# Two mixers of a hybrid decoder trunk: evacuating queries and values from PSUM at once, an order of products per mixer, and new places in the planner's queues

## The chip, the cores and the metric

The kernel runs as one program on one core of a Trainium2 chip. The metric is the device time of one execution in microseconds (us). Three runs of the kernel before took 2170.38, 2173.52 and 2178.13 us; the median is 2173.52. A change of less than 0.3% can't be told from none here.

## The reference

The reference is one inference step of a trunk of two layers with a width of 1024, for 16 meta tokens, a prompt of 512 tokens and eight running sequences of four tokens each: 560 token columns in all. Everything is float32. One layer does this:

```
h = h + 0.5 * swiglu(rmsnorm(h, norm_ffn1), ...)            # 1024 -> 2816 -> 1024
z = rmsnorm(h, norm_mix) @ w_in                             # q, f, v, gate, u: five parts of 512
q = silu(zq); log_f = log(lb + (1-lb) sigmoid(zf)); k = (1-lb) sigmoid(-zf)
o_hg = HGRN2(q, log_f, k, v)        # S_t = diag(f_t) S_{t-1} + k_t v_t^T, o_t = S_t^T q_t; 4 heads of 128
o_hg = rmsnorm(o_hg per head) * silu(zg)
y = gelu(S5(u))                     # complex diagonal scan, 32 groups of 16 columns, 64 states
y = rmsnorm(y * sigmoid(y @ w_glu + b_glu))
h = h + concat(o_hg, y) @ w_out
h = h + 0.5 * swiglu(rmsnorm(h, norm_ffn2), ...)
```

The outputs are the normalised h and the new states of the HGRN2 heads and of the S5 groups, for the prompt and for each running sequence.

## The kernel before

All arrays lie feature-major: a tile has 128 features on its partitions and the 560 tokens beside each other. Each float32 operand of the large products is cut into a high and a low part of a reduced format, and a product is the sum of three (high by high, high by low, low by high). So one product of the mixer with 1024 inputs and 128 outputs is 8 x 3 x 2 = 48 matmuls of 128x128 by 128x280, which add up in a pair of PSUM banks. Weights come from HBM over SyncE's queue (raw) and once more over GpSimd's queue, where the DMA adds the raw weight to a negated high part, so that the low part results; ScalarE makes the high parts.

Four feed-forward stages and two mixers follow each other: feed-forward, mixer 0, two feed-forwards, mixer 1, feed-forward. The feed-forward products use a scheme with seven block products for eight; the change does not touch it beyond its places.

The order of the instructions on the engines is made before the launch by a planner (`Sched`, lines 78 to 288). The work is written as tasks (Python generators), each of which yields one operation after the other, waits for events of other tasks, or asks a pool for a buffer. The planner keeps an estimated clock per engine, and for each engine takes the operation with the smallest key, which is its possible start plus a pull times the task's place:

```
key = st + PULL.get(o.eng, 0.0) * t.prio
if t.slack and o.eng in ("PE", "S"):
    key = max(key, rdy + t.slack)
```

So a place is a handicap in ns for VectorE ("V") and ScalarE ("S"), and none for TensorE and GpSimd. Engines run the emitted instructions in that order and wait at each for what it needs. Some VectorE operations may go to GpSimd (`flex`, line 335) if they end there no later than `BIAS` ns after VectorE would end them.

The pools (line 302) are: `t`, 50 SBUF tiles of 564 columns; `a`, 20 of 1024; `mm`, three pairs of PSUM banks; `m1`, two single banks. In a mixer the main task gets an `mm` pair only where another one stays free (`mtask[0].psum = 1`), so it holds two at most. The S5 and head tasks are ranked: the more of them with a better place are alive (those that wait for a PSUM pair not counted), the more `t` tiles must be free before a task gets one: `RES=(0, 6, 6, 6, 82)`. The fifth one thus gets no tile at all until another ends. A task without that mark needs no free tiles beside its own.

A mixer (`mixer`, line 1846) walks through `ORDER` (line 72), one list for both mixers: `f`, `q`, `v` and `g` with a number are the products of a head, `u` those of one of the four S5 blocks, `x` the two halves of the S5 gate (`w_glu`), which need all four S5 outputs. The weights are loaded in the same order (`wsrc`, line 488). After a product the main task spawns the task that uses it:

- `t_s5` (a block of S5) evacuates u as soon as the norm factor is known, waits for the tables of the layer (`d.ev`), sends u to DRAM and back in another layout, waits for the block before it, and then does a product, a scan on VectorE, a second product and the gelu; y goes to DRAM and back as well.
- `t_head` (line 1568) evacuates f and makes the decay and k, then waits for the q product and evacuates it, waits until the head two before it has done its levels (`prev`), does the first block product, and only then waits for the v product and evacuates it. Seven levels of pairwise decays with a block product each follow, then the states and the output.
- `t_og` applies the gate product to a head's output, `t_glu` the S5 gate, `t_yn` the norm of y. The eight output products come last; each takes the parts of its input in the order in which they are ready.

The tables of a layer's S5 blocks are made by `t_setup` (line 1247 on): some hundreds of short VectorE steps in a chain and some DMA through DRAM. That of layer 0 starts with the kernel, that of layer 1 after mixer 0.

Of the kernel before, what the change touches and what calls it, by code (L numbers as in the profile page):

```python
# [67 lines left out]
BIAS = 1000.0  # L68
# [3 lines left out]
ORDER = 'f0 u0 f1 u1 q0 u2 v0 q1 f2 u3 v1 q2 f3 q3 x0 v3 x1 v2 g1 g3 g2 g0'.split()  # L72
# [4 lines left out]
PULL = {"PE": 0.0, "V": 60.0, "S": 60.0, "G": 0.0}  # L77
# [214 lines left out]
def hymba(ctx: ExitStack, tc: tile.TileContext, *aps):  # L292
# [172 lines left out]
    for l in range(L):  # L465
        for i in ("1", "2"):
            f = 2 * l + int(i) - 1

            def put_units(a, b):
                for k in range(a, b):  # L470
                    unit_at[f, k] = len(wsrc)
                    if f or k >= PLAIN:
                        pair.add(len(wsrc))
                    wsrc.extend([(A_["gu" + i][l, k, 0], 8), (A_["gu" + i][l, k, 1], 8)])

            for a, (c, o, n) in enumerate(CH):
                put_units(ends[a] - n, ends[a])
                down_at[f, a] = len(wsrc)
                if n == 4:
                    wsrc += [(A_["dn" + i][l, c, m:m + 2, :, o:o + 4].rearrange("m p k q -> p m k q"), 8)  # L480
                             for m in range(0, KD, 2)]
                else:
                    wsrc += [(A_["dn" + i][l, c, m, :, :n], n) for m in range(KD)]
            if i == "1":
                m0 = len(wsrc)
                for w, i in ORDER:
                    i = int(i)
                    wsrc.append((A_["wglu"][l, i] if w == "x" else A_["win"][l, WIN[w] + i], 8))
                wsrc += [(A_["wout"][l, m], 8) for m in range(KD)]
                wmix.append((m0, len(wsrc)))  # L490
# [198 lines left out]
    class Norm:  # L689
        def __init__(self, nm, l, src, ev, o0=0, plain=False):  # L690
            self.rs = Ev()
            self.nm, self.l, self.src, self.ev = nm, l, list(src), ev
            self.sq = [Ev() for _ in range(KD)]
            self.o0, self.T = o0, TOK - o0
            self.fast = nm != "nm"
            if self.fast:
                self.xb = {b: [Ev() for _ in range(4)] for b in ("11", "12", "t1", "21", "22", "t2", "t3", "t4")}
                self.xt = []
                self.plain = plain
                self.order = XO if self.plain else range(KD)  # L700
                if self.plain:
                    self.x12, self.y = [], [Ev() for _ in range(KD)]
                    spawn(self.t_first(), 0.931, name="split" + nm)
                    spawn(self.t_then(), 1.2, name="sums" + nm)
                else:
                    spawn(self.t_blocks(), 0.931, name="split" + nm)
            else:
                self.order = range(KD)
                self.xs = [Ev() for _ in range(KD)]
                spawn(self.t_split(), 2.931, name="split" + nm)  # L710
            spawn(self.t_sum(), 1.9 if self.fast else 8.533, name="sum" + nm).slack = 1500.0 if self.fast else 0.0
# [138 lines left out]
    class Unit:  # L850
# [9 lines left out]
        def prod(self, j):  # L860
            w, o, b = PROD[j]
            q, i = wq[self.i], self.i
            if j == 1:
                self.x = yield am1()
                spawn(t_cuts(self), 2.45, name="cuts")
                spawn(t_hid(self), 2.452, name="hid").slack = 400.0
# [21 lines left out]
    class Plain:  # L888
# [4 lines left out]
        def run(self):  # L893
            pss = []
            for n in range(2):
# [13 lines left out]
                if not n:  # L909
                    self.f = Ev()  # L910
                    spawn(t_evac(ps, self.f), 2.45, name="cuts")
            spawn(t_phid(self, ps), 2.452, name="hid")
# [193 lines left out]
    def ffn(nrm, f, nm2, l2=0):  # L1106
# [14 lines left out]
        for u, j in prog:  # L1121
# [30 lines left out]
            for m in range(KD):  # L1152
# [3 lines left out]
                spawn(t_res(pd[m] if m < 2 else p, m, 0.5, hevs[m] if last else Ev(), o0=nrm.o0), 3.536, name="res")  # L1156
# [410 lines left out]

    def t_head(l, hd, st, ps, evs, nrm, prev, nxt, out):
        yield evs[0]
# [10 lines left out]
        yield evs[1]  # L1580
        q = yield from evac(ps[1], rs, "q")
# [33 lines left out]
        yield evs[2]  # L1615
        v = yield from evac(ps[2], rs, "v")
# [229 lines left out]
    def mixer(l, nrm):  # L1846
        spawn(t_park(nrm), 3.523, name="park")
# [17 lines left out]
        spawn(t_ysplit(ys, yh), 8.515, name="ysplit")  # L1865
        spawn(t_yn(l, y2, yf, o0), 2.578, name="yn")
        for w, i in ORDER:
            i = int(i)
            ps = yield am()
            if w == "u":  # L1870
                yield from gemm(ps, list(nrm.xs))
                spawn(t_s5(l, i, st, ps, nrm, nu[i], nu[i + 1], ys[i]), 0.477 + 0.01 * i, 1, name=f"s5{i}")
            elif w == "g":
                yield from gemm(ps, list(nrm.xs), T=TOK - o0, o0=o0)
                spawn(t_og(l, i, ps, nrm, ons[i], ogs[i], o0), 2.926, name="og")
            elif w == "x":
                for j in range(2):
# [3 lines left out]
                    spawn(t_glu(l, 2 * i + j, ps, ys[2 * i + j], y2[2 * i + j]), 2.92, name="glu")  # L1881
# [3 lines left out]
            else:  # L1885
                j = "fqv".index(w)
                hps[i][j] = ps
                if j == 0:
                    spawn(t_head(l, i, st, hps[i], hev3[i], nrm, rel[i], rel[i + 2], ons[i]), 1.202 + 0.01 * i, 1,
# [8 lines left out]
        spawn(t_unpark(back), 9.518, name="unpark")  # L1898
# [4 lines left out]
        for ms in OUT_M:  # L1903
# [9 lines left out]
            while final:  # L1913
# [15 lines left out]
                if n[a] == KD:  # L1929
                    final.remove(a)  # L1930
                    spawn(t_res(pss[a], ms[a], 1.0, hevs[ms[a]], back[ms[a]], o0), 3.536, name="res")
# [7 lines left out]
    def t_main():  # L1939
# [3 lines left out]
        for l in range(L):  # L1943
            nn = yield from ffn(nn, 2 * l, "nm", l)
            nn = yield from mixer(l, nn)
            if l + 1 < L:
                spawn(t_setup(l + 1), 8.527, name="setup")
# [6 lines left out]
    for f, pr in ((t_wload, 0.1), (t_wsplit, 2.311), (t_wsum, 2.312)):  # L1954
        spawn(f(), pr, name=f.__name__[2:])
    spawn(t_ones(), 1.5, name="ones")
    spawn(t_const(), 8.52, name="const")
    spawn(t_mask(), 8.9, name="mask")
    spawn(t_setup(0), 8.527, name="setup")
# [121 lines left out]
```

## Time and profile before

| what | value |
|---|---|
| median of three runs | 2173.52 us |
| the profiled execution's own time | 2174.55 us |
| its span, first to last instruction | 2172.7 us |
| TensorE matmul busy | 2069.9 us (95%) |
| VectorE busy | 1622.1 us (75%) |
| ScalarE busy | 1151.2 us (53%) |
| GpSimd busy | 492.4 us (23%) |
| mean granted TensorE clock | 0.979 of full speed |
| moved by DMA | 388.08 MB, mean 179 GB/s |

The profile is one execution, and times in it count from the first instruction. TensorE's granted clock has two levels, 1.2 and 2.4 GHz, shown as 0.5 and 1.0; a stretch's figure is the mean. A waiting instruction is put down to what released it. Names such as `q<-mm,rs` say what is written from what: here the evacuation of a q product from its PSUM pair, multiplied by the norm factor. `zf`, `v`, `u` and `zg` are the same for the other products, `ut,mi` is the first product of an S5 block, `xh,wh` a piece of a dense one.

### The profile page before, as it was taken

Reading aid. Unit: us, or ns where it says so; the run is one execution under the profiler, and the core shown is the slowest. Engines: PE = TensorE matmul, PEld = TensorE weight load, DVE = VectorE, ACT = ScalarE, POOL = GpSimd, SP = SyncE. Lnnn points to the kernel's source line nnn. Section 1 sums busy time; section 2 is a strip of 40 time slices with the busy share of each in tenths; the row PEclk is TensorE's granted clock in tenths of the full one; section 3 lists DMA queues with packets and bytes.
Section 4 is the critical chain, followed back from the end, with each engine's and each line's share of the span. In section 5 each row is a group of like instructions: output and inputs, shape, how many; then the busy total and the mean of one; then the engine's idle time right before and its main releaser. Section 6 shows DMA issues by size and latency. Waiting matters only on the chain.

```text
span 2172.7 us, 43858 instructions
## 1 busy us (share of the span) xinstructions
PE 2069.9 (95%) x17394; PEld 2019.2 (93%) x17394; DVE 1622.1 (75%) x3654; ACT 1151.2 (53%) x1888; POOL 492.4 (23%) x606
## 2 busy tenths in 40 slices
PE   8999999988699999999999999999988999999997
PEld 7999999987598999999999999999978889999997
DVE  8879769867577977866998865665677797566674
ACT  6556656433354645575765564554434466545563
POOL 2232232322221223123212221112221221111111
PEclk9999999989899999999999999999989999999999
DMA  7798688876456678868857876688856667667773
GB/s 206 162 227 217 154 230 185 235 208 201 109 127 188 151 168 221 196 168 208 191 127 192 217 183 158 154 203 222 216 152 151 164 140 180 169 153 171 183 178 82
DMA packets 153325, 388.08 MB, mean 179 GB/s; under 512 B 16176, under 2 KB 36432, under 8 KB 153120
## 3 DMA queue, kind: packets, MB, share of 16 engines
q0 software_dynamic: 65760, 177.27, 42.6%
q1 hardware_dynamic: 75904, 182.48, 25.4%
q10 hardware_dynamic: 11456, 25.54, 3.4%
q8 instruction: 136, 2.23, 0.4%
q14 instruction: 69, 0.57, 0.1%
HBM read 352.56 MB, written 32.67 MB: 177 GB/s over the span
## 4 chain that ended last, share of the span: by engine, by line
PE 55%; DVE 14%; issue 4%; ACT 2%; DMA 2%; POOL 1%; DVEq 0%; ACTq 0%; POOLq 0%
PE mm L408 38%; PE m L408 16%; DVE xl L333 2%; DVE wr L333 1%; DVE wl L333 1%; ACT wh L372 1%; DMA wl<-in_dn_dram 1%; DVE w L333 1%; DVE fa L333 1%; DMA smin<-mex 1%; DVE w L1523 1%; DVE qp L333 1%; DVE rv L333 1%; DVE ks L333 0%; DVE xh L364 0%
## 5 line engine op out<-in xcount | busy, mean ns | idle before, releaser
L408 PE MATMUL mm<-xh,wh 128*128 128x280 f32 (+1 forms) x3432 | 821.8, 296 | 8.9 <-ACT s L372 3.7
L408 PE MATMUL mm<-xl,wh 128*128 128x280 f32 (+1 forms) x3432 | 809.9, 292 | 6.5 <-DVE xl L333 6.5
L408 PE MATMUL mm<-xh,wl 128*128 128x280 f32 (+1 forms) x3432 | 807.6, 291 | 1.2 <-DMA wl<-in_dn_dram 1.2
L372 ACT ACTIVATE wh<-wr 128x1024 fp32r<-128x1024 f32 (+2 forms) x590 | 524.6, 915 | 285.6 <-DVE wr L333 191.5
L408 PEld LDWEIGHTS mm<-xh,wh 128*128 128x128 f32 x3432 | 577.0, 189 | 23.9 <-issue 7.4
L408 PEld LDWEIGHTS mm<-xl,wh 128*128 128x128 f32 x3432 | 578.6, 189 | 9.4 <-DVE xl L333 9.4
L408 PEld LDWEIGHTS mm<-xh,wl 128*128 128x128 f32 x3432 | 577.9, 189 | 1.7 <-DMA wl<-in_dn_dram 1.7
L408 PE MATMUL m<-xh,wh 128*128 128x280 f32 (+1 forms) x1112 | 310.8, 293 | 1.3 <-ACT fa L372 0.9
L408 PE MATMUL m<-xl,wh 128*128 128x280 f32 (+1 forms) x1032 | 300.9, 292 | 0.4 <-DVE xl L333 0.4
L408 PE MATMUL m<-xh,wl 128*128 128x280 f32 (+1 forms) x952 | 277.6, 292 | 0.3 <-DMA wl<-in_gu_dram 0.3
L372 ACT ACTIVATE wl<-wr 128x1024 fp32r<-128x1024 f32 (+1 forms) x244 | 249.2, 1021 | 40.6 <-PE mm L408 20.2
L333 DVE TENSOR_TENSOR wl<-wr,wh 128x1024 fp32r<-128x1024 f32 x174 | 212.7, 1222 | 54.5 <-PE mm L408 28.5
L333 DVE TENSOR_TENSOR wr<-wr 128x512 f32<-128x512 f32 x344 | 236.0, 686 | 16.3 <-ACT wh L372 13.8
L408 PEld LDWEIGHTS m<-xh,wh 128*128 128x128 f32 x1112 | 206.0, 189 | 4.7 <-issue 2.0
L361 DVE SCALAR_TENSOR_TENSOR h<-mm,h 128x560 f32<-128x560 f32 (+1 forms) x157 | 114.8, 735 | 127.7 <-PE mm L408 126.7
L408 PEld LDWEIGHTS m<-xl,wh 128*128 128x128 f32 x1032 | 195.2, 189 | 0.6 <-DVE xl L333 0.6
L387 POOL DMA_DIRECT2D wl<-in_gu_dram x88 | 77.4, 879 | 522.3 <-ACT wl L372 280.6
L387 POOL DMA_DIRECT2D wl<-in_dn_dram x96 | 103.7, 1082 | 348.2 <-ACT wl L372 131.3
L408 PEld LDWEIGHTS m<-xh,wl 128*128 128x128 f32 x952 | 180.2, 189 | 0.5 <-DMA wl<-in_gu_dram 0.5
L408 PE MATMUL m<-x,wh 128*128 128x280 f32 (+1 forms) x952 | 142.9, 290 | 0.0
L408 PEld LDWEIGHTS m<-x,wh 128*128 128x128 f32 x952 | 129.9, 188 | 0.2 <-issue 0.2
L387 POOL DMA_DIRECT2D wh<-in_gu_dram x86 | 75.8, 881 | 108.4 <-ACT wh L372 87.3
(321 smaller groups left out, 2391.8 us busy)
## 6 DMA issues: line engine op xcount, KB each, us to landing
wr<-in_gu_dram SPq DMA_DIRECT2D x176, 512.0 KB, 5.8
wl<-in_gu_dram POOLq DMA_DIRECT2D x88, 512.0 KB, 5.6
wr<-in_dn_dram SPq DMA_DIRECT2D x64, 512.0 KB, 4.8
wl<-in_dn_dram POOLq DMA_DIRECT2D x64, 512.0 KB, 9.5
wh<-in_gu_dram POOLq DMA_DIRECT2D x86, 256.0 KB, 6.2
wr<-in_win_dram SPq DMA_DIRECT2D x40, 512.0 KB, 6.1
wl<-in_win_dram POOLq DMA_DIRECT2D x40, 512.0 KB, 7.8
wr<-in_dn_dram SPq DMA_DIRECT2D x32, 384.0 KB, 5.4
```

Of the source, the lines that this page charges most:

```text
L333: return Op("V" if e is V else "G", c, [o], [a, b], lambda: e.tensor_tensor(o, a, b, op=op), port=sb(a, b))
L361: lambda: V.scalar_tensor_tensor(o, a, s, b, op0=op0, op1=op1), port=sb(a, b))
L372: return Op("S", nel(o) * 0.833 + (190 if sc else 95 if sb(a) else 60), [o], [a] + sc, lambda: S.activation(o, a, func, scale=scale, **kw))
L387: return Op("G", 900.0, [o], [i, o], lambda: G.dma_start(o, i, accum_op=ALU.add), lat=-n / 240.0)
L408: PE.matmul(out, lhsT=lhsT, rhs=rhs, start=st, stop=sp_, **kw)
L1523: yield vop(a, [a, d.r4], lambda a=a, dk=dk: V.tensor_tensor_scan(a, dk, a, 0.0, op0=ALU.mult, op1=ALU.add))
```

## The change

The order of products becomes a pair of lists, one for each mixer, in which the gates stand last; the weights are loaded in the same orders. A new task, `t_take`, is spawned twice for each head. It waits for its product (q or v) and for the norm factor, evacuates the product into a tile of pool `t`, and sets an event, for which the head waits where it evacuated before. Its place is 0.00 to 0.03, ahead of all others, and it has no mark for the tile reserve. The rest are numbers: `BIAS` 722.5 for 1000, the pulls 35.7 (VectorE) and 51.0 (ScalarE) for 60, and the places of most tasks. The diff, with the context cut:

```diff
-BIAS = 1000.0
+BIAS = 722.5
...
-ORDER = 'f0 u0 f1 u1 q0 u2 v0 q1 f2 u3 v1 q2 f3 q3 x0 v3 x1 v2 g1 g3 g2 g0'.split()
+ORDER = ('f0 u0 u1 q0 v0 f1 u2 f2 q1 v1 u3 q2 f3 q3 v2 v3 x0 x1 g1 g2 g0 g3'.split(), 'f0 u0 q0 u1 f1 v0 u2 q1 u3 v1 f2 f3 q2 q3 x1 x0 v2 v3 g2 g0 g1 g3'.split())
...
-PULL = {"PE": 0.0, "V": 60.0, "S": 60.0, "G": 0.0}
+PULL = {"PE": 0.0, "V": 35.7, "S": 51.0, "G": 0.0}
...
-                for w, i in ORDER:
+                for w, i in ORDER[l]:
...
-                    spawn(self.t_first(), 0.931, name="split" + nm)
-                    spawn(self.t_then(), 1.2, name="sums" + nm)
+                    spawn(self.t_first(), 0.183, name="split" + nm)
+                    spawn(self.t_then(), 1.756, name="sums" + nm)
...
-                    spawn(self.t_blocks(), 0.931, name="split" + nm)
+                    spawn(self.t_blocks(), 0.687, name="split" + nm)
...
-                spawn(self.t_split(), 2.931, name="split" + nm)
-            spawn(self.t_sum(), 1.9 if self.fast else 8.533, name="sum" + nm).slack = 1500.0 if self.fast else 0.0
+                spawn(self.t_split(), 8.104, name="split" + nm)
+            spawn(self.t_sum(), 1.4 if self.fast else 1.493, name="sum" + nm).slack = 3672.0 if self.fast else 0.0
...
-                spawn(t_cuts(self), 2.45, name="cuts")
-                spawn(t_hid(self), 2.452, name="hid").slack = 400.0
+                spawn(t_cuts(self), 0.629, name="cuts")
+                spawn(t_hid(self), 2.684, name="hid").slack = 18.203
...
-                    spawn(t_evac(ps, self.f), 2.45, name="cuts")
-            spawn(t_phid(self, ps), 2.452, name="hid")
+                    spawn(t_evac(ps, self.f), 15.971, name="cuts")
+            spawn(t_phid(self, ps), 10.356, name="hid")
...
-                spawn(t_res(pd[m] if m < 2 else p, m, 0.5, hevs[m] if last else Ev(), o0=nrm.o0), 3.536, name="res")
+                spawn(t_res(pd[m] if m < 2 else p, m, 0.5, hevs[m] if last else Ev(), o0=nrm.o0), 4.172, name="res")
...
+    def t_take(ev, ps, j, nrm, out):
+        yield ev
+        yield nrm.rs
+        out.val = yield from evac(ps[j], nrm.rs.val, "qv")
+        out.done = True
...
+        qq, vv = Ev(), Ev()
+        spawn(t_take(evs[1], ps, 1, nrm, qq), 0.0 + 0.01 * hd, name="take")
+        spawn(t_take(evs[2], ps, 2, nrm, vv), 0.0 + 0.01 * hd, name="take")
...
-        yield evs[1]
-        q = yield from evac(ps[1], rs, "q")
+        yield qq
+        q = qq.val
...
-        yield evs[2]
-        v = yield from evac(ps[2], rs, "v")
+        yield vv
+        v = vv.val
...
-        spawn(t_park(nrm), 3.523, name="park")
+        spawn(t_park(nrm), 4.399, name="park")
...
-        spawn(t_ysplit(ys, yh), 8.515, name="ysplit")
-        spawn(t_yn(l, y2, yf, o0), 2.578, name="yn")
-        for w, i in ORDER:
+        spawn(t_ysplit(ys, yh), 15.455, name="ysplit")
+        spawn(t_yn(l, y2, yf, o0), 5.762, name="yn")
+        for w, i in ORDER[l]:
...
-                spawn(t_s5(l, i, st, ps, nrm, nu[i], nu[i + 1], ys[i]), 0.477 + 0.01 * i, 1, name=f"s5{i}")
+                spawn(t_s5(l, i, st, ps, nrm, nu[i], nu[i + 1], ys[i]), 0.0 + 0.01 * i, 1, name=f"s5{i}")
...
-                spawn(t_og(l, i, ps, nrm, ons[i], ogs[i], o0), 2.926, name="og")
+                spawn(t_og(l, i, ps, nrm, ons[i], ogs[i], o0), 5.71, name="og")
...
-                    spawn(t_glu(l, 2 * i + j, ps, ys[2 * i + j], y2[2 * i + j]), 2.92, name="glu")
+                    spawn(t_glu(l, 2 * i + j, ps, ys[2 * i + j], y2[2 * i + j]), 6.774, name="glu")
...
-                    spawn(t_head(l, i, st, hps[i], hev3[i], nrm, rel[i], rel[i + 2], ons[i]), 1.202 + 0.01 * i, 1,
+                    spawn(t_head(l, i, st, hps[i], hev3[i], nrm, rel[i], rel[i + 2], ons[i]), 2.79 + 0.01 * i, 1,
...
-        spawn(t_unpark(back), 9.518, name="unpark")
+        spawn(t_unpark(back), 6.354, name="unpark")
...
-                    spawn(t_res(pss[a], ms[a], 1.0, hevs[ms[a]], back[ms[a]], o0), 3.536, name="res")
+                    spawn(t_res(pss[a], ms[a], 1.0, hevs[ms[a]], back[ms[a]], o0), 0.0, name="res")
...
-                spawn(t_setup(l + 1), 8.527, name="setup")
+                spawn(t_setup(l + 1), 9.809, name="setup")
...
-    for f, pr in ((t_wload, 0.1), (t_wsplit, 2.311), (t_wsum, 2.312)):
+    for f, pr in ((t_wload, 0.1), (t_wsplit, 3.082), (t_wsum, 2.458)):
...
-    spawn(t_const(), 8.52, name="const")
+    spawn(t_const(), 4.719, name="const")
...
-    spawn(t_setup(0), 8.527, name="setup")
+    spawn(t_setup(0), 7.136, name="setup")
...
```

## Rows read from the trace of the kernel before

**Rows 1.** The page, parts 1 and 2: busy shares; granted clock in 40 slices.

```profile
PE 2069.9 (95%) x17394; PEld 2019.2 (93%) x17394; DVE 1622.1 (75%) x3654; ACT 1151.2 (53%) x1888; POOL 492.4 (23%) x606
...
PEclk9999999989899999999999999999989999999999
```

**Rows 2.** Windows: length, engines' busy us (instructions), granted clock, DMA share, GB/s.

```profile
418.90:724.00 305.10, 266.17 (x2712) 249.40 (x2710) 225.26 (x603) 126.47 (x242) 69.45 (x89) 0.93 0.63 164
724.00:1105.00 381.00, 377.38 (x2940) 371.63 (x2940) 306.75 (x714) 228.29 (x379) 99.67 (x126) 1.00 0.78 189
1155.00:1485.00 330.00, 327.35 (x2532) 326.39 (x2531) 234.07 (x472) 178.83 (x259) 60.33 (x72) 1.00 0.75 181
1503.30:1787.70 284.40, 258.67 (x2722) 242.81 (x2720) 211.11 (x479) 128.26 (x241) 68.65 (x81) 0.96 0.67 171
1800.00:2150.00 350.00, 348.98 (x2783) 348.75 (x2782) 223.55 (x355) 193.78 (x290) 63.56 (x66) 1.00 0.70 164
0.00:30.00 30.00, 19.23 (x76) 16.60 (x77) 23.05 (x50) 23.88 (x36) 8.86 (x13) 0.89 0.96 291
552.10:586.80 34.70, 17.23 (x207) 15.18 (x207) 20.80 (x49) 8.60 (x25) 8.78 (x11) 0.80 0.37 103
2150.00:2172.70 22.70, 9.69 (x76) 8.60 (x74) 14.62 (x48) 4.50 (x10) 0.00 (x0) 0.77 0.29 99
```

**Rows 3.** Waits of TensorE, 440 to 760: us in total, times, longest.

```profile
PE mm L408 <- POOL xs L333: 11.5, 2, 9.8
```

**Rows 4.** The chain that ended last: start us, us, what.

```profile
1453.35 41.24 PE mm L408 x318
```

**Rows 5.** Time line of TensorE, mixer 0: start us, us, instruction, wait before.

```profile
465.75 0.42 PE L408 MATMUL mm<-xh,wl 128*128 128x280 f32 x2
466.10 0.45 PE L408 MATMUL m<-qp,ks 128*32 128x32 f32 x16
481.08 0.53 PE L408 MATMUL mm<-xh,wh 128*128 128x280 f32 x2 [1.70 <-ACT ksv L372]
```

**Rows 6.** Time line of VectorE, mixer 0: evacuations of q, u, f, v.

```profile
471.31 0.73 DVE L333 TENSOR_TENSOR q<-mm,rs 128x560 f32<-128x560 f32 x1
515.09 0.72 DVE L333 TENSOR_TENSOR zf<-mm,rs 128x560 f32<-128x560 f32 x1
566.41 0.73 DVE L333 TENSOR_TENSOR zf<-mm,rs 128x560 f32<-128x560 f32 x1
601.59 0.74 DVE L333 TENSOR_TENSOR v<-mm,rs 128x560 f32<-128x560 f32 x1
616.55 0.73 DVE L333 TENSOR_TENSOR v<-mm,rs 128x560 f32<-128x560 f32 x1
```

**Rows 7.** Time lines of several engines: S5 in both mixers, end of mixer 0.

```profile
456.28 0.57 POOL L383 DMA_DIRECT2D stt<-ti  x1
472.72 2.07 PE L408 MATMUL mm<-ut,mi 128*128 128x140 f32 x8
550.21 1.12 PE L408 MATMUL mm<-ut,mi 128*128 128x140 f32 x8
585.14 0.45 DVE L364 CAST xh<-y 128x560 fp32r<-128x560 f32 x1
722.06 0.73 DVE L333 TENSOR_TENSOR h<-mm,h 128x560 f32<-128x560 f32 x1
1504.45 1.29 DVE L333 TENSOR_TENSOR u<-mm,rs 128x16 f32<-128x16 f32 x4 [0.38 <-PE mm L408]
1519.13 1.07 PE L408 MATMUL mm<-ut,mi 128*128 128x140 f32 x7
1589.83 0.28 DVE L333 TENSOR_TENSOR u<-mm,rs 128x16 f32<-128x16 f32 x2
1606.34 1.11 PE L408 MATMUL mm<-ut,mi 128*128 128x140 f32 x8
```

**Rows 8.** Waits of VectorE, 418.9 to 724: us in total, times, longest.

```profile
DVE u L333 <- PE mm L408: 5.6, 3, 2.7
```

## The prediction

> **What bounds the kernel now.** I read the page first, then a table by stage, then the waits and the time lines of the two mixers. TensorE is busy 95% of the span, so only its idle time and its slow time can be won [rows 1]. The table by stage puts both in few places [rows 2]. In the three feed-forward stretches TensorE is busy 377.4 of 381, 327.4 of 330 and 349.0 of 350 us at full clock: 7 us in all. Mixer 0 (from the first evacuation at 418.9 to 724) has it busy 266.2 of 305.1 us at a mean granted clock of 0.93, mixer 1 258.7 of 284.4 us at 0.96. That is 38.9 and 25.7 us idle. A mean of 0.93 between the levels 1.0 and 0.5 costs at most 0.07 of the busy time, 19 us, and 0.96 costs 10 us. So mixer 0 can give back 58 us at most and mixer 1 36 us. The start adds 10.8 us of idle time and the end 13.0 [rows 2], and the change reorders little there.
>
> Why mixer 0 idles shows in its time lines. A dense product (48 matmuls) takes 6.2 us: 318 matmuls in 41.24 us, 0.13 us each [rows 4]. The main task issues the products in one order, and may hold only two of the three large PSUM pairs. Nine products were done at 466.1; the tenth, u3, began at 481.08 [rows 5], because q1 sat in its pair until 471.31 and f2 until 515.09 [rows 6]. Later x0, in its place in the order, waited for the last S5 block: y was split at 585.14 [rows 7], and in 552.1 to 586.8 TensorE was busy 17.2 of 34.7 us at 0.80 [rows 2], the longest wait in it being for the last S5 block's POOL sums, 9.8 us [rows 3]. Six products that need only the normalised input (v3, v2, four gates) stood behind x0 all this time; v was evacuated at 601.59 and 616.55 [rows 6].
>
> The S5 blocks were late for a reason of their own: the last table of the layer's setup was stored at 456.28, and the first S5 product came at 472.72, while mixer 1, whose tables were long there, had it at 1519.13, 14.7 us after its first u at 1504.45 [rows 7]. In mixer 0 that distance is 472.72 less 418.9, 53.8 us: 39 us are setup. The four S5 blocks then follow at (550.21 less 472.72) / 3 = 25.8 us [rows 7].
>
> **The change part by part.**
>
> *Takes.* Eight multiplications per mixer (four q, four v, 0.73 us each [rows 6]) move from the head into tasks of their own at the front of VectorE's ranking. None is added: work 0. What they buy is that q and v leave PSUM when their product ends and not when the head comes to them. f products are not taken: f2 and f3 still wait until a head may start (f2 waited 49 us, 466 to 515 [rows 5, 6]). So the main task stops next where f2 and f3 fill its two pairs: in the new order of mixer 0 before its 14th product, in mixer 1 before its 13th, in place of the 10th. The new wait stands on VectorE: a take placed too early holds its queue until TensorE ends the product. The u evacuations, placed the same way, held it 5.6 us in 3 times, 2.7 at most [rows 8]; eight takes thus cost 0 to 22 us of VectorE per mixer, behind which S5 and head steps queue. VectorE idles 305.1 - 225.3 = 80 and 284.4 - 211.1 = 73 us there [rows 2], so I take 0 on the path; without that cover it would be up to 22.
>
> *Order of mixer 0.* v2 and v3 go ahead of x0: 12.4 us of dense work moves into the stretch 552.1 to 586.8, where TensorE had 17.5 us free [rows 2]. Between the end of x0's wait and the last addition to h (722.06 [rows 7]) stand 135 us, with 15.5 products (96 us) before the change: x0 and x1 less the half that ran early, v3, v2, four gates, eight of the output. Afterwards 14 (87 us): -9 us, between 0 and -12.
>
> *Places: setup.* A task's place times the pull (ns) is its handicap against others' start times. On VectorE setup's goes from 8.527 x 60 = 512 to 7.136 x 35.7 = 255, that of the hidden products from 147 to 96, of the residual additions from 212 to 149. Setup is a long chain of short steps on an engine about 80% busy there, so a smaller gap (300 to 106 behind the residual additions) lets it slip in sooner. From no gain (tables still at 456) to all 39 us; I take half, 20, since x0 cannot profit from a start earlier than the main task reaches it: 16 products and the heads' part lie before. Mixer 0: -9 and -20, less 3 for TensorE's other limits: -26, leaving 279 us, 32 above its floor of 247.
>
> *Order of mixer 1.* x1 and x0 still stand before v2 and v3, so nothing moves past that wait. But u3 comes 9th and not 10th, and no q or v blocks it. It was evacuated at 1589.83 and its S5 product ran at 1606.34 [rows 7]; at 25.8 us each the fourth would be due at 1519.1 + 77.4 = 1596.5. That is 10 us of S5 chain, and x follows it: -11 with a stall or two of the heads; bounds 0 and -25.
>
> *All other places* (splits, sums, residual additions, norms, the weights' sums), the lower bias (POOL takes a step only if it ends less than 0.72 us later, not 1.0) and the pulls shift steps against each other in feed-forward stretches. No instruction or DMA is added; DMAs of the parked h, the S5 round trips and the weight loads keep their queues but follow their tasks. The cover is TensorE's dense work, 99% of these stretches. Nothing to win over 7 us there, perhaps 3 at either end; if a split or weight split comes late TensorE waits for it. I take +3, between -8 and +10.
>
> *Sum.* The profiled execution took 2174.55 us (span 2172.70). -26 - 11 + 3 = -34: 2140.5. The median of the runs shown is 1 us below it, so 2140.
>
> *A rule of the Trainium skill against this.* Granted clock is 0.80 where TensorE was half busy and 1.00 in the dense stretches [rows 2]. The Trainium skill ("TensorE: Matmul & The Clock Gate", "What's actually happening") says that throttled is the default and activity releases it. The trace agrees. By it, dense products that are only run earlier leave a sparser stretch behind, and the slow time moves instead of going; the clock's share of the gain, about a third of it, would then be lost and the time would be near 2151, inside the range.
>
> **The rivals.**
>
> *No change.* Setup stays late, x0 is released near 587 as before, and f2 and f3 fill the pairs a little later than q1 and f2 did. For it: f2's 49 us in PSUM, untouched by the takes. Against it: the hole before x0 that v2 and v3 can now fill. Price: -9 in mixer 0, -2 in mixer 1, +6 elsewhere: 2169.
>
> *Slower: the takes use up SBUF tiles.* A take asks for a tile of the pool of 50 with no reserve, while S5 blocks and heads keep one. In a mixer 16 tiles hold the split input and one the norm; q and v of heads 2 and 3 now lie there unused until those heads start. If S5 blocks wait for tiles, each of the four comes later. At 8 us a block, the fourth is 24 late and x0 with it: +24 - 9 in mixer 0, nothing gained and about +5 in mixer 1: +20, 2194. It decides once the S5 blocks of mixer 0 follow at more than 30 us, or once the last y is split after 595. Against it: both heads and S5 blocks run two deep in the trace without such a stall on view.
>
> *Larger.* Setup done before mixer 0, and both mixers near their floors: -44 and -25: 2105. For it: the floors (58 and 36). Against it: heads and S5 chains are long rows of short dependent steps, and gates still stand behind x0.
>
> **How the numbers follow.** Forecast 0.60 (its own range 2120 to 2160), no change 0.18, slower 0.11, larger 0.11. A measurement of this kernel tells 0.3% (6.5 us) from no change. Faster by more: 0.60 + 0.11 + half of the no-change case = 0.80; within it 0.07; slower 0.11 + 0.02 = 0.13. The range 2110 to 2176 leaves out the slower case and half of the larger one.
>
> **What would show it.** Right: evacuations of q1 and v1 within some 5 us of their products; v2 and v3 in mixer 0 evacuated before the last y is split; the last setup table stored before about 440, the first S5 product before 460; mixer 0 near 279 us and mixer 1 near 273; the clock in the first above 0.95. Wrong: setup's last table still after 450, S5 blocks more than 30 us apart, new TensorE waits for splits in the feed-forward stretches of more than 10 us, or a hole before x0 as long as the old one.

## The result and the profile after

The changed kernel took 2094.36 us (median of four runs, 2091.69 to 2095.2) against 2171.95 for the kernel before on the same chip: a ratio of 0.9644, interval 0.9626 to 0.9662. The forecast was 2140, with a range down to 2110. It went the way of the "larger" rival (2105) and 11 us beyond.

The page of the changed kernel, parts 1 and 2, against [rows 1]:

```profile
PE 2039.8 (97%) x17394; PEld 1996.7 (95%) x17394; DVE 1622.6 (78%) x3681; ACT 1152.5 (55%) x1875; POOL 468.7 (22%) x592
...
PEclk9999999999999999999999999999999999999998
```

The number of matmuls is the same and their busy time fell by 30 us. The windows of the two mixers (from the first evacuation to the last addition to h), of a dense stretch, the start and the end; columns as in [rows 2]:

```profile
416.00:675.40 259.40, 250.22 (x2704) 236.45 (x2703) 213.31 (x543) 122.97 (x236) 63.14 (x81) 0.99 0.74 196
1449.30:1710.10 260.80, 248.52 (x2703) 234.75 (x2702) 206.28 (x469) 129.97 (x242) 64.87 (x81) 0.99 0.71 185
1085.00:1430.00 345.00, 345.00 (x2674) 344.83 (x2673) 248.11 (x496) 192.78 (x281) 65.30 (x78) 1.00 0.77 185
0.00:30.00 30.00, 20.79 (x103) 17.70 (x104) 25.46 (x64) 24.85 (x39) 5.25 (x11) 0.89 0.84 272
2070.00:2092.80 22.80, 8.79 (x69) 7.70 (x67) 14.37 (x47) 3.73 (x9) 0.00 (x0) 0.74 0.29 98
```

Mixer 0 went from 305.1 to 259.4 us, mixer 1 from 284.4 to 260.8 [rows 2]. Of the 45.7 us in mixer 0, idle time gave 29.7 (38.9 to 9.2) and busy time 16.0 (266.2 to 250.2, the clock from 0.93 to 0.99); of the 23.6 in mixer 1, 13.4 and 10.2. The new windows hold 8 and 19 matmuls fewer than those of [rows 2]; for the same number the busy time fell by about 15 and 8 us. The dense stretch is busy throughout at full clock, and the start and the end hardly moved. The largest group of TensorE's waits in mixer 0 (total, times, longest) is now this, where [rows 3] had 9.8 us in one:

```profile
PE m L408 <- DVE ktt L333: 2.0, 2, 1.6
```

The time lines of the changed kernel: the stage borders (last additions to h), then mixer 0 in the order of the prediction's steps (last setup table; first and fourth S5 product; last dense matmul and evacuation of q1, then of v1; v2 and v3; last y split):

```profile
404.17 0.74 DVE L361 SCALAR_TENSOR_TENSOR h<-mm,h 128x560 f32<-128x560 f32 x1
674.71 0.73 DVE L333 TENSOR_TENSOR h<-mm,h 128x560 f32<-128x560 f32 x1
1437.48 0.74 DVE L361 SCALAR_TENSOR_TENSOR h<-mm,h 128x560 f32<-128x560 f32 x1 [1.71 <-PE mm L408]
1709.41 0.72 DVE L333 TENSOR_TENSOR h<-mm,h 128x544 f32<-128x544 f32 x1
...
433.96 0.57 POOL L383 DMA_DIRECT2D stt<-ti  x1
450.55 1.22 PE L408 MATMUL mm<-ut,mi 128*128 128x140 f32 x8
516.69 1.19 PE L408 MATMUL mm<-ut,mi 128*128 128x140 f32 x8
471.14 0.42 PE L408 MATMUL mm<-xh,wl 128*128 128x280 f32 x2
471.60 0.74 DVE L333 TENSOR_TENSOR qv<-mm,rs 128x560 f32<-128x560 f32 x1
484.09 0.42 PE L408 MATMUL mm<-xh,wl 128*128 128x280 f32 x2
485.72 0.73 DVE L333 TENSOR_TENSOR qv<-mm,rs 128x560 f32<-128x560 f32 x1
539.64 0.73 DVE L333 TENSOR_TENSOR qv<-mm,rs 128x560 f32<-128x560 f32 x1
550.42 0.74 DVE L333 TENSOR_TENSOR qv<-mm,rs 128x560 f32<-128x560 f32 x1 [1.05 <-PE mm L408]
551.55 0.74 DVE L333 TENSOR_TENSOR xl<-y,xh 128x560 fp32r<-128x560 f32 x1
```

With the stage borders all runs can be set side by side. Mixer 0 is the second row less the first, and so on; these figures begin a few us before the windows above, at the end of the stage before. All in us; every ratio below is to the kernel before on the same chip. The stages are those of one execution each, so 2 or 3 us in a stage prove nothing: ten executions of e18 lay between 2160.34 and 2177.19. The medians come from several chips, on which the kernel before took 2168.08 to 2172.51.

| kernel | before mixer 0 | mixer 0 | between | mixer 1 | end | median |
|---|---|---|---|---|---|---|
| before | 405.0 | 317.0 | 768.7 | 296.8 | 385.2 | 2171.95 |
| changed | 404.2 | 270.5 | 762.8 | 271.9 | 383.4 | 2094.36 |
| numbers only (e1) | 405.9 | 288.8 | 763.5 | 295.7 | 386.4 | 2142.17 |
| orders only (e2) | 403.9 | 306.0 | 769.6 | 281.0 | 383.6 | 2146.89 |
| orders and takes (e3) | 403.8 | 303.9 | 769.3 | 281.8 | 386.4 | 2149.56 |
| orders and numbers, no takes (e4) | 405.1 | 289.3 | 763.1 | 280.9 | 382.4 | 2124.98 |
| before, setup earlier (e5) | 406.7 | 293.8 | 770.3 | 299.2 | 383.3 | 2151.22 |
| changed, setup late (e6) | 401.1 | 347.8 | 765.2 | 272.1 | 382.2 | 2169.88 |
| changed, mixer 0's list twice (e7) | 404.1 | 270.0 | 764.9 | 271.0 | 383.0 | 2096.0 |
| changed, setup earlier (e8) | 439.3 | 269.7 | 762.9 | 270.1 | 383.3 | 2125.57 |
| changed, S5 and heads' places old (e9) | 405.0 | 279.1 | 765.3 | 278.6 | 382.3 | 2110.72 |
| changed, places behind heads old (e10) | 403.4 | 283.8 | 761.1 | 284.2 | 384.9 | 2125.25 |
| changed, pulls old (e11) | 422.0 | 291.0 | 775.9 | 284.8 | 382.4 | 2156.5 |
| changed, setup at 8.5 (e12) | 403.4 | 279.3 | 762.4 | 272.3 | 383.2 | 2105.92 |
| e3 with places behind heads new (e13) | 403.8 | 307.9 | 769.9 | 270.9 | 384.6 | 2141.06 |
| changed, q's take only (e14) | 402.8 | 293.7 | 763.4 | 282.2 | 383.2 | 2126.63 |
| changed, v's take only (e15) | 410.1 | 284.5 | 764.8 | 271.5 | 383.5 | 2109.7 |
| e4 with a smaller reserve (e16) | 404.3 | 274.4 | 763.2 | 279.5 | 383.7 | 2106.72 |
| changed, smaller reserve (e17) | 406.5 | 273.2 | 764.0 | 274.5 | 384.3 | 2104.88 |
| before, smaller reserve (e18) | 403.6 | 317.5 | 768.8 | 296.5 | 383.7 | 2173.18 |

The change gave 46.5 us in mixer 0, 24.9 in mixer 1 and 8.5 elsewhere (5.9 of them between the mixers): 79.9, the difference of the spans.

### The profile page after: what moved, and what is told of

Read it like the earlier page. It is cut to its first block, busy times and chain, and to the rows that moved or that the text cites. A ratio compares the mean times of both kernels' runs of the same rounds, so it can differ in the third digit from the quotient of the medians.

```text
span 2092.8 us, 43860 instructions
## 1 busy us (share of the span) xinstructions
PE 2039.8 (97%) x17394; PEld 1996.7 (95%) x17394; DVE 1622.6 (78%) x3681; ACT 1152.5 (55%) x1875; POOL 468.7 (22%) x592
## 4 chain that ended last, share of the span: by engine, by line
PE 83%; DVE 10%; DMA 3%; ACT 2%; issue 2%; POOL 0%; SPq 0%; ACTq 0%; DVEq 0%; POOLq 0%
PE mm L408 57%; PE m L408 25%; DVE xl L333 1%; DVE w L333 1%; DVE wr L333 1%; DVE wl L333 1%; DMA smin<-mex 1%; DMA wl<-in_dn_dram 0%; ACT wh L372 0%; DVE w L1523 0%; DVE sq L333 0%; DMA gb<-in_bt_dram 0%; DVE xh L364 0%; DVE qp L333 0%; DMA tpl<-stp 0%
```

## The experiments

### The parts: numbers, orders, takes

The change has three parts: the orders, the takes, and the numbers (places, pulls, bias). The theories were that the numbers do it, or that the PSUM pairs freed by orders and takes do it.

The numbers alone (e1):

```diff
-ORDER = ('f0 u0 u1 ...'.split(), 'f0 u0 q0 ...'.split())
+ORDER = ('f0 u0 f1 u1 q0 u2 v0 ...'.split(),) * 2
-        spawn(t_take(evs[1], ...
-        spawn(t_take(evs[2], ...
```

> The kernel before with all numbers of the change (pulls, places, bias), but neither the takes nor the new orders: q and v are evacuated by the heads, and both mixers use the old list. Theory A (the places: S5 and setup run earlier, the rest follows) expects most of the 80 us: 2172 less 45 to 65, so 2107 to 2127, with the first S5 product of mixer 0 before 455 and the clock in the mixers above 0.97. Theory B (PSUM: takes and order keep dense products at hand, the places add the setup's share) expects 2172 less 20 to 25, about 2150, with q1 and f2 still lying in PSUM for tens of us.

Measured: 0.988 of before (0.9849 to 0.991), 30 us. Nearly all of it is mixer 0 (-28.2); mixer 1 has -1.1.

The orders alone (e2), in the kernel before:

```diff
-ORDER = 'f0 u0 f1 u1 q0 u2 v0 ...'.split()
+ORDER = ('f0 u0 u1 ...'.split(), 'f0 u0 q0 ...'.split())
-        for w, i in ORDER:
+        for w, i in ORDER[l]:
```

> The kernel before with the two new orders of products alone: old numbers, no takes. Theory B expects -10 to -20 (v2 and v3 go into the hole before x0 of mixer 0, mixer 1 nearly unchanged): 2152 to 2162. Theory A expects -10 at most, since S5 stays as late as before and x0 is released near 587: 2162 to 2172.

Measured: 0.9898 (0.9871 to 0.9925), 26 us: 11.0 in mixer 0, 15.8 in mixer 1. With the numbers beside them (e4 against e1) the orders are worth nothing in mixer 0 (+0.5) and as much in mixer 1 (-14.8).

Orders and takes without the numbers (e3): e2 with `t_take` and its two spawns.

> The kernel before with the new orders and the takes, old numbers. Theory B expects 55 of the 80 us, 2115 to 2120, the setup's 20 us missing in mixer 0 alone and mixer 1 near 262 us as in the changed kernel. Theory A expects 2145 to 2165: mixer 1 stays above 272 us, because S5 and the heads keep their old places.

Measured: 0.9906 (0.987 to 0.9943). The takes add nothing here: -2.1 and +0.8. In e2 and e3 alike the last setup table comes 12 us later than in [rows 7], so mixer 0 pays for later tables in both. In e2:

```profile
467.98 0.57 POOL L383 DMA_DIRECT2D stt<-ti  x1
```

The changed kernel without the takes (e4):

```diff
-        spawn(t_take(evs[1], ...
-        spawn(t_take(evs[2], ...
-        yield qq
+        yield evs[1]
+        q = yield from evac(ps[1], rs, "q")
-        yield vv
+        yield evs[2]
+        v = yield from evac(ps[2], rs, "v")
```

> The changed kernel without the takes: q and v are evacuated by the heads as before; orders and numbers are the new ones. Theory B expects 25 to 40 us lost against the changed kernel, 2120 to 2135, as q and v again hold PSUM pairs. Theory A expects under 12 us lost, 2094 to 2106.

Measured: 0.9792 (0.9767 to 0.9818). Here the takes are missed: +18.8 in mixer 0, +9.0 in mixer 1. Neither theory holds by itself. The numbers give 30, the orders 26, orders and numbers 48, all three 78: the takes pay only beside the other two. There is no kernel with takes in the old order: all tiles of pool `t` are held there, and the plan can't go on. So what the takes give beside the numbers alone is not known.

### Setup's place

```diff
-    spawn(t_setup(0), 7.136, name="setup")
+    spawn(t_setup(0), 2.0, name="setup")     # e8; 8.5 in e12, 14.3 in e6
```

In the kernel before, and nothing else (e5):

```diff
-    spawn(t_setup(0), 8.527, name="setup")
+    spawn(t_setup(0), 3.0, name="setup")
```

> The kernel before with one number changed: setup of layer 0 at place 3.0 (180 ns on VectorE) in place of 8.527 (512 ns). If the late tables are what the numbers cured in mixer 0 (28 us of it with the numbers alone), the last table is stored before 430, the first S5 product runs near 435 to 450 and the time falls by 18 to 28 us: 2145 to 2155. The rival, that S5's and the heads' own places did it, expects -8 at most: 2164 to 2172.

Its last table and its first S5 product:

```profile
425.15 0.90 POOL L383 DMA_DIRECT2D stt<-ti  x1
...
446.98 1.12 PE L408 MATMUL mm<-ut,mi 128*128 128x140 f32 x8
```

Measured: 0.9914 (0.9893 to 0.9934). The table is 31 us earlier than in [rows 7], mixer 0 shorter by 23.2 us, and little else gains. That is the term of the prediction (20), measured by itself, though with a handicap of 180 ns where the change has 255.

In the changed kernel, setup late (e6):

> The changed kernel with setup of layer 0 at place 14.3, the 510 ns on VectorE that it had before. If the tables bind mixer 0, its last table comes after 450 and mixer 0 loses what the table is later, 10 to 22 us: 2104 to 2117. If other places did it: 2092 to 2098.

Measured: 1.0004 (0.9989 to 1.0019): the whole gain is gone, far beyond what was expected. The last table came at 525 and mixer 0 took 347.8 us. Setup's handicap is the old one here (510 ns), and in the kernel before its table came at 456: what a place is worth hangs on the places of the others. TensorE's waits in e6 from 400 to 760 (total, times, longest):

```profile
PE mm L408 <- ACT ksv L372: 21.3, 7, 12.2
PE mm L408 <- DVE tm L333: 12.5, 1, 12.5
```

The second one is a step of the setup itself.

Setup earlier still (e8):

> The changed kernel with setup of layer 0 at place 2.0 (71 ns on VectorE; 255 in the changed kernel). If mixer 0 still waits for tables (last one at 434, first S5 product at 451), the first S5 product moves to 430 to 440 and the time falls by 3 to 12 us: 2082 to 2091. If mixer 0 is by now bound by TensorE (250 of 259 us busy): 2092 to 2097.

Measured: 0.9793 (0.9773 to 0.9813). The last table came at 326.8, mixer 0 gained 0.8 us, and the feed-forward before it lost 35. TensorE's waits in e8 from 0 to 420:

```profile
PE mm L408 <- DMA wl<-in_dn_dram: 11.3, 3, 8.3
PE mm L408 <- DVE xh L364: 7.8, 1, 7.8
```

TensorE waits there for weights and splits. Setup's place is all that differs from the changed kernel, so they must have stood behind setup's steps; the trace was not followed that far. Setup at 8.5 (e12):

> The changed kernel with setup of layer 0 at place 8.5 (303 ns on VectorE, 255 in the changed kernel). Setup at 2.0 cost 35 us ahead of mixer 0, at 14.3 it won 3 us there and cost 77 in mixer 0. If the table at 434 has slack, this wins 1 to 3 us: 2091 to 2094. If it has none, each us of a later table costs 0.8: 2095 to 2115.

Measured: 0.9703 (0.9678 to 0.9728). Tables at 326.8, 434.0, 450.0 and 525.0 give a mixer 0 of 269.7, 270.5, 279.3 and 347.8: nothing ahead of about 434, then 0.5 to 0.9 us for each us. The new place is late enough to spare the feed-forward and just early enough.

### Mixer 1's own list

```diff
-ORDER = ('f0 u0 u1 ...'.split(), 'f0 u0 q0 ...'.split())
+ORDER = ('f0 u0 u1 ...'.split(), 'f0 u0 u1 ...'.split())
```

> The changed kernel with mixer 0's list of products for both mixers (in mixer 1 v2 and v3 then stand before the S5 gate products). If a list of its own is worth something to mixer 1, it loses 3 to 10 us there: 2097 to 2104. If v2 and v3 ahead of x help there as they were expected to in mixer 0: 2085 to 2094.

Measured (e7): 0.9663 (0.9636 to 0.969), mixer 1 271.0 against 271.9. Whether v2 and v3 stand ahead of x0 makes no difference there, nor does a list of its own.

### The numbers part by part

Old places for S5 blocks and heads (e9):

```diff
-                spawn(t_s5(...), 0.0 + 0.01 * i, 1, name=f"s5{i}")
+                spawn(t_s5(...), 0.477 + 0.01 * i, 1, name=f"s5{i}")
-                    spawn(t_head(...), 2.79 + 0.01 * i, 1,
+                    spawn(t_head(...), 1.202 + 0.01 * i, 1,
```

> The changed kernel with the old places of S5 blocks (0.477) and heads (1.202). Open: which number makes the takes pay, since with the old numbers they gave 0 in both mixers and with the new ones 19 us in mixer 0 and 9 in mixer 1. Theory H1 (it is the lead of S5 over the heads) expects 10 to 28 us lost, 2104 to 2122, mixer 1 near 281. If it is another number: under 6 us, 2090 to 2100.

Measured: 0.9726 (0.9703 to 0.975): +8.6 and +6.7 in the mixers.

Old places for the tasks behind the heads (e10):

```diff
-                spawn(t_og(...), 5.71, name="og")
+                spawn(t_og(...), 2.926, name="og")
-                    spawn(t_glu(...), 6.774, name="glu")
+                    spawn(t_glu(...), 2.92, name="glu")
...                                                     # park, ysplit, yn, unpark, res too
```

> The changed kernel with the old places of what follows S5 and heads in a mixer: S5 output split 8.515, y norm 2.578, gates 2.926, S5 gates 2.92, residual additions of the mixer 3.536, park 3.523, unpark 9.518. Theory H2 (these tasks crowd the heads' steps when they rank ahead) expects 10 to 28 us lost, 2104 to 2122, in both mixers. Otherwise under 6 us: 2090 to 2100.

Measured: 0.9796 (0.9769 to 0.9822): +13.3 and +12.3. The outputs of the last head of each mixer are normalised at these times, first in e10, then in the changed kernel:

```profile
641.91 0.80 DVE L361 SCALAR_TENSOR_TENSOR on<-on,pk,rs 128x560 f32<-128x560 f32 x1 [1.38 <-ACT rs L372]
1687.77 0.80 DVE L361 SCALAR_TENSOR_TENSOR on<-on,pk,rs 128x560 f32<-128x560 f32 x1 [1.28 <-ACT rs L372]
```

```profile
632.26 0.78 DVE L361 SCALAR_TENSOR_TENSOR on<-on,pk,rs 128x560 f32<-128x560 f32 x1
1667.08 0.80 DVE L361 SCALAR_TENSOR_TENSOR on<-on,pk,rs 128x560 f32<-128x560 f32 x1 [2.44 <-ACT rs L372]
```

In mixer 0 the head is 10 us later, though the last y is split no later than in the changed kernel (550.67 against 551.55). With old places, gates (2.926) and heads (2.79) are nearly equal. Two of the four gates of mixer 0 are then evacuated 11 us earlier than in the changed kernel (195.1 and 206.9 us after the stage's start against 206.5 and 217.4), and the last two heads are normalised 8 and 10 us later. That fits gates that take VectorE and ScalarE from the heads, which end last; the edit moves seven kinds of task at once, and which of them does it was not tried.

The old pulls (e11):

```diff
-PULL = {"PE": 0.0, "V": 35.7, "S": 51.0, "G": 0.0}
+PULL = {"PE": 0.0, "V": 60.0, "S": 60.0, "G": 0.0}
```

> The changed kernel with both pulls at 60 as before. All handicaps on VectorE grow by 1.68. Theory H3 (the flatter ranking on VectorE makes the takes pay) expects 10 to 28 us lost in the mixers. Setup's handicap becomes 428 ns, so its last table should come later than 434 and cost mixer 0 some of that in any case: 2100 to 2125. If neither: 2090 to 2098.

Measured: 0.9935 (0.9913 to 0.9958), the dearest single edit but e6: +20.5 and +12.9 in the mixers, +17.8 ahead of them and +13.1 between. The pull scales all places at once, so this run doesn't say which of them it is.

New places for the tasks behind the heads, in e3 (e13):

```diff
-                spawn(t_og(...), 2.926, name="og")
+                spawn(t_og(...), 5.71, name="og")
...                                                     # the others of e10 too
```

> The kernel before with new orders, takes and the new places of what follows S5 and heads in a mixer (output split, y norm, gates, S5 gates, the mixer's residual additions, park, unpark); all other numbers old. If these places are what makes the takes pay, mixer 1 falls from 281.8 us (orders and takes alone) to 270 to 274 and the time from 2149.6 to some 2130. If it takes the lead of S5 and the flatter pulls as well, mixer 1 stays above 277: 2142 to 2150.

Measured: 0.9867 (0.9851 to 0.9883). Mixer 1 goes from 281.8 to 270.9: beside the takes these places win 11 us there, with no other number changed. Without takes they stand in e4, among the other new numbers, and mixer 1 takes 280.9 us, as long as with the orders alone (281.0 in e2). So it takes both, unless another of e4's numbers hides a gain; these places alone, without takes, were not run. Mixer 0 stays at 307.9; its last table comes at 468, as in e2 and e3.

### What a take is worth, and by what

The changed kernel with the take of q only (e14) and of v only (e15); the other product is evacuated in the head, as in e4's diff:

> The changed kernel with takes of q alone; v is evacuated by the head again. v leaves PSUM only after the head's first block product, so if v is what held the pairs, most of the 31 us that the takes are worth is lost: 2115 to 2126. If q did: 2094 to 2105.

> The changed kernel with takes of v alone; q is evacuated by the head again. If v is what held the pairs: 2094 to 2105. If q did (q2 and q3 wait for heads that have not started): 2115 to 2126. If either alone holds a pair as long as both, both runs lose over 20 us.

Measured: 0.9801 (0.9783 to 0.982) and 0.9726 (0.9705 to 0.9747). In mixer 1 v's take is the whole gain (271.5 with it, 282.2 without). Mixer 0 needs both: 293.7 and 284.5 against 270.5.

In mixer 0 a take frees a PSUM pair. The product of q2, the 12th in the list, ends near 508 in e4, without takes, and in the changed kernel. In e4 q2 and f3 then lie in the main task's two pairs until the heads come to them, and between the 13th product and the next there is no dense matmul for 35 us. The last one before, the two evacuations, the first one behind, and the window between:

```profile
513.62 0.42 PE L408 MATMUL mm<-xh,wl 128*128 128x280 f32 x2
544.51 0.73 DVE L333 TENSOR_TENSOR q<-mm,rs 128x560 f32<-128x560 f32 x1
545.16 0.73 DVE L333 TENSOR_TENSOR zf<-mm,rs 128x560 f32<-128x560 f32 x1
548.80 0.52 PE L408 MATMUL mm<-xh,wh 128*128 128x280 f32 x2
514.00:548.80 34.80, 19.11 (x255) 16.18 (x254) 24.97 (x64) 7.43 (x22) 7.58 (x10) 0.66 0.34 104
```

In the changed kernel q2 leaves as its product ends, and the gap is 4 us:

```profile
507.84 0.73 DVE L333 TENSOR_TENSOR qv<-mm,rs 128x560 f32<-128x560 f32 x1
512.96 0.43 PE L408 MATMUL mm<-xh,wl 128*128 128x280 f32 x2
517.63 0.51 PE L408 MATMUL mm<-xh,wh 128*128 128x280 f32 x2
```

Mixer 1 is different. Head 1 shows what v's take changes there: v is evacuated, and the head begins its levels (`qp<-qp,f`). First the changed kernel, then e4, without takes:

```profile
1525.55 0.73 DVE L333 TENSOR_TENSOR qv<-mm,rs 128x560 f32<-128x560 f32 x1
1531.49 0.45 DVE L333 TENSOR_TENSOR qp<-qp,f 128x280 f32<-128x280 f32 x1
```

```profile
1546.92 0.73 DVE L333 TENSOR_TENSOR v<-mm,rs 128x560 f32<-128x560 f32 x1
1583.29 0.44 DVE L333 TENSOR_TENSOR qp<-qp,f 128x280 f32<-128x280 f32 x1
```

6 us against 36, though v leaves PSUM equally late in both (76 and 78 us after the mixer's first evacuation). So it is not v's pair that comes free earlier. Between the two rows the head asks for tiles of pool `t` and for a pair to transpose in. A ranked head gets a tile only where more than 6 are free, while a take's tile is outside that reserve. In the plan of e4, whose times are the planner's estimates, head 1 waits 26 us for a tile with exactly 6 free, and then 1 us for a pair, while f2 and f3 lie in theirs until heads 2 and 3 get a tile. In mixer 0 of the same plan head 2 stands 19 us for a tile with 6 free before it comes to q2. The trace of e4 has mixer 1's f2 and f3 evacuated together, as the plan has them; in the changed kernel they are 14 us apart, at 1553.84 and 1567.74:

```profile
1574.21 1.38 DVE L333 TENSOR_TENSOR zf<-mm,rs 128x560 f32<-128x560 f32 x2
```

That reading was put to the test with a smaller reserve, without takes (e16), in the changed kernel (e17) and in the kernel before (e18):

```diff
-RES = (0, 6, 6, 6, 82)
+RES = (0, 3, 3, 3, 82)
```

> The changed kernel without its takes (q and v evacuated in the head, as before) and with the tile reserve RES 3 for 6: a ranked task gets a tile of pool t as soon as more than 3 are free, not 6. The e4 kernel, the same with 6, took 2125 us (mixers 289.3 and 280.9 us); the changed kernel 2094 (270.5 and 271.9). Theory T, tiles: what the takes are worth is mostly that a head no longer stands for a tile under the reserve, since a take's tile is outside it. In e4's mixer 1 head 1 evacuated v at 1546.92 and began its levels only at 1583.29, 36 us later, against 6 us with the take of v alone. Then the lower reserve does much of the same without a take: head 1 of mixer 1 starts its levels within 15 us of its v, the mixers take 272 to 280 and 270 to 275 us, the run 2095 to 2110. Theory P, PSUM: the takes are worth what the pairs are worth that come free early; a reserve of SBUF tiles changes nothing in that, and the run stays at 2118 to 2128 with mixers of 286 to 291 and 278 to 283.

Measured: 0.9722 (0.9695 to 0.9748), by the ratios 15 us faster than with a reserve of 6. Mixer 0 gets back 14.9 of its 18.8 us: q2 leaves its pair at 514.83, and the gap behind the 13th product is 7 us. Mixer 1 gets back 1.4 of 9.0, and its head 1, in e16, halves its delay to 18 us:

```profile
1531.52 0.73 DVE L333 TENSOR_TENSOR v<-mm,rs 128x560 f32<-128x560 f32 x1
1549.55 0.42 DVE L333 TENSOR_TENSOR qp<-qp,f 128x280 f32<-128x280 f32 x1
```

So in mixer 0 the two theories are one: under the reserve head 2 stands without a tile, so q2 stays in its pair and the main task stops; a take or a smaller reserve empties the pair. In mixer 1 the reserve is part of head 1's delay, but hardly of the time of the mixer. The dense products stop there for 17 us behind the 12th in e4 and for no more than 7 at a time in e16, and little is won by that. Counted from the stage's start, the last two heads are normalised at 229.7 and 237.5 us in e16, at 217.7 and 229.6 in the changed kernel. What that hangs on stays open.

> The changed kernel, with takes, and RES 3 for 6. Theory T: the takes have gone round the reserve already, and little is left: 2086 to 2097 us, with mixers of 264 to 271 and 268 to 272. Theory P expects no change: 2092 to 2097. A time above 2100 would say that the reserve protects the S5 blocks and heads with a better place, and that lowering it costs more than it frees.

Measured: 0.9708 (0.9689 to 0.9727), 10 us slower than the changed kernel by the medians and 14 by the ratios: with the takes the reserve has its use, as the last sentence of the expectation had it. In the one execution traced, 2.7 and 2.6 us of it are in the mixers and the rest around them.

> The kernel before with RES 3 for 6 and nothing else. Theory T: the reserve holds heads up here too, but S5 comes late in mixer 0 and the old order puts six products behind x0 in both mixers, so only a part shows: 2150 to 2166 us. Theory P: no change, 2168 to 2174.

Measured: 1.0018 (0.9999 to 1.0038), no change; theory T had expected a gain. The reserve was not what limited the kernel before.

No kernel tried beats the changed one; e7 equals it.

## Why the prediction fell short

**The bound and the places to win** were right: both mixers, and nearly nothing else. The floors (58 and 36 us) held; 46 and 24 of them were won.

**Setup (-20)** came near in size, by the mechanism named: -23.2 by itself (e5). Tables before 440 and S5 before 460 came as named (433.96, 450.55).

**Order of mixer 0 (-9, v2 and v3 ahead of x0)** was near for the kernel before alone (-11.0 in e2, with later tables). Beside the new numbers it is worth nothing (e4 against e1: +0.5). In e1 the last y is split 30 us earlier than in the kernel before (the low part, below, at 587.28 there; the high part is in [rows 7]), and with it a part of the hole ahead of x0 is gone without v2 and v3. In e4 a hole of 35 us stands before the 14th product instead, until a take empties q2's pair. In e1:

```profile
557.41 0.73 DVE L333 TENSOR_TENSOR xl<-y,xh 128x560 fp32r<-128x560 f32 x1
```

The prediction added the two terms, -9 and -20; measured without takes, they don't add up.

**Order of mixer 1 (-11)** was low: -15.8 by itself. Its reason was partly wrong: it rested on u3's place and on q and v not blocking, and e2 has the gain with no take. It doesn't come from the list being mixer 1's own (e7).

**Takes (0 on the path)** is the first step that failed. The VectorE hold was priced well: in mixer 0 VectorE waited 5.2 of the 22 us allowed for products in front of the takes (VectorE's waits in the changed kernel):

```profile
DVE qv L333 <- PE mm L408: 5.2, 3, 3.7
```

q1 and v1 left within 0.1 and 1.3 us of their last matmul (471.14 and 484.09, each 0.42 long). But the takes got no gain of their own. The prediction let the main task stop before the 14th product of mixer 0, at f2 and f3, with them. In the changed kernel f2 is evacuated at 470.2, 8 us behind its product and not 49, and the stop before the 14th product is 4 us; without takes it is q2 and f3 that fill the pairs, for 35 us (e4). The takes' worth beside the rest is 18.8 and 9.0 us. The tile reserve, which keeps the heads from q2 in mixer 0, stood in the prediction with the opposite sign: the slower rival had the takes starving S5 of tiles. Its points from which it decides were not met: S5 blocks follow at (516.69 - 450.55) / 3 = 22.0 us, not over 30, and the last y is split at 551.55, not after 595.

**All other places (+3)** is the second. They were priced in the feed-forward stretches and the ends alone, where they gave 8.5 us (bound -8). Inside the mixers the same numbers decide which of the waiting tasks gets VectorE and ScalarE: undone singly, the places of S5 and heads cost 15.3 us there, those behind the heads 25.6. The prediction gave them no term there; it counted 80 and 73 us of idle VectorE in the mixers as cover for the takes, but that is a sum over the mixer, and the head that ends last waits for its turn at single steps (e10). These costs are measured beside the takes; without them the numbers, setup's place included, won 28.2 us in mixer 0 and 1.1 in mixer 1 (e1).

**The clock.** The slow time went and didn't move: it is 0.99 in both mixers. The Trainium skill's rule ("TensorE: Matmul & The Clock Gate", "What's actually happening") agrees with that in so far as the engine is busy 96% and 95% there; the case that was weighed by it, a sparser stretch left behind, didn't come about.

In sum, mixer 0 gave 46.5 for 26, mixer 1 24.9 for 11, and the rest 8.5 where 3 had been expected to be lost. Of the 46 us missed, the takes are 28, the stages outside the mixers 11, and the mixers without takes (e4) 5 and 2. Without the takes mixer 0 gave 27.7, close to the 26. That is luck in part, for the order's 9 did not come and the numbers gave 28. The chance of 0.11 for the larger case was too small. Its argument against was that heads and S5 are long rows of short steps. That does not speak against a gain: which of the waiting steps gets an engine, a tile or a pair first is what the change moves; the work stayed the same.

## What to carry to other kernels

Idle time of an engine, summed over a stage, is no cover for priorities: ask which chain ends last in the stage and who stands before it at each of its steps. Parts of a change that free the same chain neither add up nor fall out one by one: measure them singly and in pairs. Where a main task stops for a buffer, ask what the task that should empty it waits for: here a head without an SBUF tile held a PSUM pair, and with it TensorE's dense work.

## What had not been expected of the hardware

The clock's share of the gain was most of its upper bound: about 15 and 8 us of busy time for the same number of matmuls, where a mean of 0.93 and 0.96 had allowed at most 19 and 10. Else nothing: the rest lies in the order of the instructions.
